# Split fetch buffers and one two-step-ahead sequence of modulation rows in a two-layer trunk

## The chip, the cores and the metric

The kernel runs on one core of a Trainium2 chip. The metric is the device time of one execution in microseconds (us); the time of a kernel is the median of its runs.

## The reference

Two layers over 512 positions of width 1024 in float32. A vector c sets, for each layer, six modulation rows of 1024 numbers:

```
ada_in = jax.nn.silu(c)
for i in range(DEPTH):
    mod = (ada_in @ w_ada[i] + b_ada[i]).reshape(b, 6, d)
    sh_m, sc_m, g_m = mod[:, 0, None, :], mod[:, 1, None, :], mod[:, 2, None, :]
    sh_f, sc_f, g_f = mod[:, 3, None, :], mod[:, 4, None, :], mod[:, 5, None, :]
    hm = rmsnorm(x, norm_mix[i]) * (1 + sc_m) + sh_m
    y = dilated_mixer(...) if i == 0 else forgetting_mixer(...)
    x = x + g_m * y
    hf = rmsnorm(x, norm_ffn[i]) * (1 + sc_f) + sh_f
    x = x + g_f * hierarchical_moe(hf, ...)
```

The dilated mixer (layer 0) projects hm to 9216 columns (three head groups of 16 heads, q, k and v each), attends within each group, merges the groups by their softmax denominators and projects back. The forgetting mixer (layer 1) is plain causal attention with a decay. The mixture of experts picks two of 16 small SwiGLU experts for each position.

## The kernel before

**Stages.** `begin` makes the first two modulation rows and the first normed input, `mixer_a` is the dilated mixer, then come the experts of layer 0, `mixer_b` and the experts of layer 1. In `mixer_a` the projection is done in four quarters Q of four heads for each group; the attention of one quarter (`far` for groups 1 and 2, `near` for group 0) is woven between the projection's matmuls by `weave`, which advances a main generator and a side generator.

**Weights.** Weights come in pieces of 128x1024 numbers (512 KB), in the order of `plan`. `Stream.fetch` puts a piece into a buffer if its counts in `held` allow one, and issues the load on SP's queue. `split` makes of a piece a high part on ScalarE (`hi`, L150) and a low part on VectorE (`lo`, L151); then the piece's buffer is free. A product is three matmuls: high by high (L302), high by low (L303), low by high (L305). A projection of 512 columns over four position blocks uses four pieces with 24 matmuls each; they are given back one after the other while the fourth block is worked on, and `done` then splits the next piece and fetches another.

**Modulation rows.** Ten more rows of `mod` are made while `mixer_a` runs. `background` lists a generator `ada` for each, and `weave` advances the first of the list at every second step of its main generator. One such row is 12 steps: eight load 128x1024 of w_ada (L400, SP's queue) and add it, times a column of silu(c), into `acc` on VectorE (L401). Then `acc` is split (L406 on ScalarE into a buffer of the weights, L407 on VectorE into `nlo`), three steps pass, and four matmuls with a column of ones add up the partitions (L413 high, L416 low). The sum goes into `nrow` and from there to memory (L423). POOL clears `acc` before (L396) and loads the bias into its first row (L397).

**Buffers.** Buffers of tag `raw` are four. Outside the experts `fetch` holds at most three for weights, and `ada` takes what is left, one at a time as a rule. The compiler's scheduler sets each engine's order from the order of the code, the dependencies and the free buffers; each engine and each queue then works in that order.

Of the kernel before, what the change touches and what calls it, by code (L numbers as in the profile page):

```python
# [8 lines left out]
F32 = mybir.dt.float32  # L9
F32R = mybir.dt.float32r  # L10
BF16 = mybir.dt.bfloat16
I32 = mybir.dt.int32
AF = mybir.ActivationFunctionType
OP = mybir.AluOpType
# [3 lines left out]
P = 128  # L18
D = 1024
S = 512  # L20
KT = D // P
# [56 lines left out]
class Stream:  # L78
# [3 lines left out]
    def __init__(self, t, pieces):  # L82
        self.t, self.pieces = t, pieces
        self.nf = self.ns = self.ng = self.nd = 0
        self.raws, self.parts = {}, {}
        self.held = {"raw": 0, "h": 0, "big": 0, "mix": 0, "row": 0, "acc": 0}
        self.moe = self.mix = self.hold = False
        self.nh = self.nrow = self.live = 0
        self.whole = {}

    def fetch(self):

        if self.nf == len(self.pieces):
            return False
        src, n, kind = self.pieces[self.nf]
        t, new = self.t, lambda pool, tag, n: pool.tile([P, 1024], F32, name=tag, tag=tag, bufs=n)
        moe = kind in ("moe", "down")
        if self.mix and kind != "" and self.held["mix"] < 6:
            tag, raw = "mix", new(t.k, "mix", 6)
        elif moe and self.held["h"] < self.nh:  # L100
            tag, raw = "h", new(t.k, "h", 8)
        elif self.moe and moe and self.held["big"] < 5:
            tag, raw = "big", new(t.k, "big", 5)
        elif moe and self.held["row"] < self.nrow:
            tag, raw = "row", new(t.k, "row", 2)
        elif self.moe and moe and self.held["acc"] < 1:
            tag, raw = "acc", new(t.w, "acc", 1)
        elif self.held["raw"] < (4 if self.moe else 3):
            tag, raw = "raw", self.t.w.tile([P, 1024], F32, name="raw", tag="raw", bufs=4)
        else:  # L110
            return False
        self.held[tag] += 1
        for ap, view in src:
            self.t.nc.sync.dma_start(out=view(raw), in_=ap)
        self.raws[self.nf] = (tag, raw)
        self.nf += 1
        return True

    def fill(self, most=10 ** 6):

        def fetch():
            while self.nf < most and self.fetch():
                pass

        fetch()
        while not self.hold and self.ns < self.nf and (self.live < 6 or self.pieces[self.ns][2] == "down"):
            self.split()
            fetch()
# [47 lines left out]
class Trunk:  # L176
# [71 lines left out]
    def finish(self):  # L248
        while self.bg:
            self.drain(self.bg.pop(0))  # L250

    def drain(self, side):
        for _ in side:
            pass
# [133 lines left out]
            if half == 0:  # L388
                self.st.fill(2)

    def ada(self, layer, j, norm, put):

        nc, i = self.nc, self.i
        acc = self.w.tile([P, D], F32, name="acc", tag="acc", bufs=1)
        row = self.nrow
        nc.gpsimd.memset(acc, 0.0)  # L396
        nc.gpsimd.dma_start(out=acc[0:1, :], in_=i["b_ada"][layer:layer + 1, j * D:(j + 1) * D])  # L397
        for kt in range(KT):
            raw = self.w.tile([P, 1024], F32, name="ada", tag="raw", bufs=4)
            nc.sync.dma_start(out=raw, in_=i["w_ada"][layer, kt * P:(kt + 1) * P, j * D:(j + 1) * D])  # L400
            nc.vector.scalar_tensor_tensor(acc, raw, self.csil[:, kt:kt + 1], acc, op0=OP.mult, op1=OP.add)  # L401
            if norm is not None and kt == KT // 2:
                nc.sync.dma_start(out=row, in_=self.bcast(norm, D, 1))
            yield
        hi, lo = self.w.tile([P, 1024], F32R, name="ada", tag="raw", bufs=4), self.nlo
        nc.scalar.activation(hi, acc, AF.Copy)  # L406
        nc.vector.tensor_tensor(lo, acc, hi.bitcast(F32), op=OP.subtract)  # L407
        for _ in range(3):
            yield
        ts = [self.bank("s")[0:1, :], self.bank("s")[0:1, :]]  # L410
        for h in range(2):
            cs = slice(h * 512, (h + 1) * 512)
            nc.tensor.matmul(ts[h], lhsT=self.one, rhs=hi[:, cs], start=True, stop=False)  # L413
        for h in range(2):
            cs = slice(h * 512, (h + 1) * 512)
            nc.tensor.matmul(ts[h], lhsT=self.one, rhs=lo[:, cs], start=False, stop=True)  # L416
        for h in range(2):
            cs = slice(h * 512, (h + 1) * 512)
            if norm is not None:
                nc.vector.scalar_tensor_tensor(row[:, cs], ts[h], 1.0, row[:, cs], op0=OP.add, op1=OP.mult)  # L420
            else:
                nc.scalar.activation(row[:, cs], ts[h], AF.Copy)
        nc.scalar.dma_start(out=put, in_=row)  # L423
        if (layer, j) == (0, 2):
            self.g_m = self.load_row(layer, 2)

    def normed(self, x, a, sh, out, sq, eng=None, after=None):

# [216 lines left out]
    def mixer_a(self, sb, xs):  # L645
# [4 lines left out]
        nc, i, st = self.nc, self.i, self.st  # L650
# [6 lines left out]
        def heads(gr):  # L657
# [15 lines left out]
            return (qt, kt, vr), turn  # L673

        def attend(near, qkv, bias, mn, den, evac):


# [82 lines left out]
        def near(Q, qkv, oqs):  # L760
            bias = sb.tile([P, 4, 256], F32, name="bias", tag="bias", bufs=2)
            nc.scalar.dma_start(out=bias, in_=bass.AP(
                tensor=ext0.tensor, offset=ext0.offset + Q * 4 * 384, ap=[[1, P], [384, 4], [1, 256]]))
            ox = sb.tile([P, NB, 264], F32, name="ox", tag="ox", bufs=1)

            def evac(hp, o):
                nc.scalar.activation(ox[:, :, 0:256].rearrange("p b (h d) -> p h b d", d=HD)[:, 2 * hp:2 * hp + 2], o, AF.Copy)

            yield from attend(True, [qkv], bias, lambda h, b: ox[:, b, 256 + h:257 + h], lambda h, b: ox[:, b, 260 + h:261 + h], evac)

            op = sb.tile([P, NB, 264], F32, name="op", tag="op", bufs=1)
            for b in range(NB):
                nc.sync.dma_start(out=near_d[Q % 2, NB - 1 - b], in_=ox[:, b, :])
            yield
            for s in range(4):
                nc.sync.dma_start(out=op[:, 3 - s, :], in_=near_d[Q % 2].rearrange("b (n r) c -> r (b n) c", r=4)[s])
            yield
            yield

            oq, st = oqs[Q]  # L780
            v = lambda n: self.sm.tile([P, NB, 4], F32, name="mg%d" % n, tag="mg%d" % n, bufs=1)
            m0, d0, m1, d1 = op[:, :, 256:260], op[:, :, 260:264], st[:, 0], st[:, 1]
            m, e0, e1, t, u = (v(n) for n in range(5))
            nc.vector.tensor_tensor(m, m0, m1, op=OP.min)
            nc.vector.tensor_tensor(e0, m, m0, op=OP.subtract)
            nc.vector.tensor_tensor(e1, m, m1, op=OP.subtract)
            nc.scalar.activation(e0, e0, AF.Exp)
            nc.scalar.activation(e1, e1, AF.Exp)
            nc.vector.tensor_tensor(t, e0, d0, op=OP.mult)
            nc.vector.tensor_tensor(u, e1, d1, op=OP.mult)  # L790
            nc.vector.tensor_tensor(t, t, u, op=OP.add)
            nc.vector.reciprocal(t, t)
            nc.vector.tensor_tensor(e0, e0, t, op=OP.mult)
            nc.vector.tensor_tensor(e1, e1, t, op=OP.mult)
            w4 = lambda a: a.unsqueeze(3).to_broadcast([P, NB, 4, HD])
            o0 = op[:, :, 0:256].rearrange("p b (h d) -> p b h d", d=HD)
            o1 = oq.rearrange("p b (h d) -> p b h d", d=HD)
            nc.gpsimd.tensor_tensor(o0, o0, w4(e0), op=OP.mult)
            nc.vector.tensor_tensor(o1, o1, w4(e1), op=OP.mult)
            nc.vector.tensor_tensor(o1, o1, o0, op=OP.add)  # L800
            yield
# [533 lines left out]
    def background(self):  # L1335
        i = self.i
        jobs = [(1, 1, i["norm_mix"][1]), (1, 0, None), (0, 2, None), (0, 3, None), (0, 4, i["norm_ffn"][0]), (0, 5, None),
                (1, 2, None), (1, 3, None), (1, 4, i["norm_ffn"][1]), (1, 5, None)]
        self.bg = [self.ada(l, j, n, self.mods[l, j:j + 1]) for l, j, n in jobs]

    def mix_in(self, layer, b, sb, x, a, sh):
        h = sb.tile([P, D], F32, name="hm", tag=("xh", "xl")[b % 2], bufs=2)
# [74 lines left out]
```

## Time and profile before

| | |
|---|---|
| median of 3 runs | 1422.62 us (1422.11 to 1424.69) |
| profiled execution | 1429.67 us, span 1427.8 us |
| PE busy | 1334.4 us, 93% |
| DVE busy | 967.1 us, 68% |
| ACT busy | 651.9 us, 46% |
| mean DMA rate | 185 GB/s |

The span is that of the recorded instructions. PE is TensorE's matmuls, PEld its weight loads, DVE VectorE, ACT ScalarE, POOL GpSimd, SP the sync engine, which here only issues loads and stores. A q behind an engine is its sequencer. "A <- B: us, n" in a view of waits says that A stood idle n times, us in total, and that the event which ended this came from B.

### The profile page before, as it was taken

How to read it: one execution, taken by the hardware profiler on the slowest of the kernel's cores; microseconds unless marked ns; L12 is line 12 of the kernel's file. 1: busy time of each engine (PE TensorE's matmuls, PEld its weight loads, DVE VectorE, ACT ScalarE, POOL GpSimd, SP SyncE). 2: the span in 40 equal slices, each digit the busy share in tenths (PEclk: the TensorE clock that was granted, in tenths of full speed). 3: DMA queues.
4: the chain of work that ended last, by engine and by line, in shares of the span. 5: the costliest groups of instructions: out<-in, count | busy, mean ns of one | idle time of the engine just before them, and what ended most of it. 6: DMA issues, size and time to landing. Idle time of an engine off the chain costs nothing. (4 is left out here: it accounts for less than half of the span.)

```text
span 1427.8 us, 20196 instructions
## 1 busy us (share of the span) xinstructions
PE 1334.4 (93%) x7165; PEld 1081.9 (76%) x7165; DVE 967.1 (68%) x1913; ACT 651.9 (46%) x1356; POOL 122.5 (9%) x120
## 2 busy tenths in 40 slices
PE   5899999999998999989999998599999999999995
PEld 4787989878996989878776665268988878766663
DVE  6875666675666676665677775486767854877772
ACT  6433544343444443453355554354554543365551
POOL 0000000000000000000032221100000000213221
PEclk9899999989999999999999999799999999999998
DMA  9465445634555545174689998513312465799991
GB/s 356 141 207 180 145 147 156 210 113 143 163 155 172 180 150 178 60 230 154 249 278 294 296 284 236 169 33 111 109 48 82 133 203 169 267 304 293 286 288 31
DMA packets 187157, 264.16 MB, mean 185 GB/s; under 512 B 23065, under 2 KB 148697, under 8 KB 187047
## 3 DMA queue, kind: packets, MB, share of 16 engines
q1 hardware_dynamic: 160742, 227.86, 49.2%
q0 software_dynamic: 8576, 16.85, 5.1%
q10 hardware_dynamic: 17728, 18.05, 4.1%
q8 instruction: 60, 0.98, 0.3%
q14 instruction: 51, 0.41, 0.1%
HBM read 249.85 MB, written 25.43 MB: 193 GB/s over the span
## 5 line engine op out<-in xcount | busy, mean ns | idle before, releaser
L302 PE MATMUL ps_pj<-hi,h 128*128 128x512 f32 (+1 forms) x1016 | 390.2, 393 | 9.6 <-ACT h L385 5.0
L303 PE MATMUL ps_pj<-lo,h 128*128 128x512 f32 (+1 forms) x1016 | 371.0, 373 | 0.0
L305 PE MATMUL ps_pj<-hi,h 128*128 128x512 f32 (+1 forms) x1016 | 288.6, 372 | 0.4 <-DVE h L463 0.4
L302 PEld LDWEIGHTS ps_pj<-hi,h 128*128 128x128 f32 x1016 | 237.5, 234 | 33.4 <-ACT h L462 7.0
L303 PEld LDWEIGHTS ps_pj<-lo,h 128*128 128x128 f32 x1016 | 239.2, 235 | 14.5 <-issue 1.1
L305 PEld LDWEIGHTS ps_pj<-hi,h 128*128 128x128 f32 x1016 | 210.7, 234 | 20.5 <-DVE h L463 1.2
L150 ACT ACTIVATE hi<-raw 128x1024 fp32r<-128x1024 f32 x126 | 132.4, 1052 | 122.6 <-PE ps_pj L305 72.0
L151 DVE TENSOR_TENSOR lo<-raw,hi 128x1024 fp32r<-128x1024 f32 x126 | 151.4, 1212 | 38.1 <-ACT hi L150 37.6
L401 DVE SCALAR_TENSOR_TENSOR acc<-ada,csil,acc 128x1024 f32<-128x1024 f32 x80 | 102.6, 1282 | 76.0 <-DMA ada<-in_w_ada 75.8
L302 PE MATMUL ps_pj<-hi,xh 128*112 128x512 f32 x256 | 103.5, 404 | 0.5 <-ACT xh L462 0.5
L303 PE MATMUL ps_pj<-lo,xh 128*112 128x512 f32 x256 | 103.3, 403 | 0.0
L305 PE MATMUL ps_pj<-hi,xl 128*112 128x512 f32 x256 | 80.3, 395 | 0.0
L1246 DVE SCALAR_TENSOR_TENSOR y<-ps_s,r_ws,g_f 112x512 f32<-112x512 f32 x64 | 47.9, 748 | 35.6 <-PE ps_s L1245 35.6
L462 ACT ACTIVATE xh<-ps_t 128x448 fp32r<-128x448 f32 x64 | 31.6, 542 | 86.4 <-PE ps_t L457 86.4
L471 DVE TENSOR_REDUCE qss<-sq 128x8 f32<-128x512 f32 x64 | 43.6, 682 | 29.9 <-ACT sq L469 29.2
L469 ACT ACTIVATE sq<-ps_pj 128x512 f32<-128x512 f32 x63 | 37.1, 588 | 55.7 <-PE ps_pj L305 53.5
L151 DVE TENSOR_TENSOR lo<-h,hi 128x1024 fp32r<-128x1024 f32 x42 | 51.1, 1222 | 15.4 <-ACT hi L150 11.2
L731 PEld LDWEIGHTS ps_o<-vr,pt 128*128 128x128 f32 x480 | 58.1, 192 | 1.4
L731 PE MATMUL ps_o<-vr,pt 128*128 128x64 f32 x480 | 57.4, 271 | 0.0
L305 PEld LDWEIGHTS ps_pj<-hi,xl 128*112 128x112 f32 x256 | 44.4, 174 | 15.2 <-DVE xl L463 0.6
L302 PEld LDWEIGHTS ps_pj<-hi,xh 128*112 128x112 f32 x256 | 44.9, 176 | 13.1 <-ACT xh L462 0.9
L936 DVE CUSTOM_DVE_ANT_0 nl<-ps_s,cums 128x128 f32<-128x128 f32 (+1 forms) x64 | 30.9, 484 | 35.2 <-PE ps_s L934 34.7
(284 smaller groups left out, 2228.4 us busy)
## 6 DMA issues: line engine op xcount, KB each, us to landing
ada<-in_w_ada SPq DMA_DIRECT2D x85, 512.0 KB
raw<-in_a_w_in SPq DMA_DIRECT2D x128, 256.0 KB
h<-in_w_gate SPq DMA_DIRECT2D x42, 256.0 KB
h<-in_w_up SPq DMA_DIRECT2D x42, 256.0 KB
mix<-in_w_gate SPq DMA_DIRECT2D x37, 256.0 KB
mix<-in_w_up SPq DMA_DIRECT2D x37, 256.0 KB
raw<-in_w_down SPq DMA_DIRECT2D x18, 512.0 KB
h<-in_w_down SPq DMA_DIRECT2D x18, 512.0 KB
```

The lines of the kernel that those rows point to most:

```text
L150: t.act = nc.scalar.activation(h, r, AF.Copy)
L151: nc.vector.tensor_tensor(l, r, h.bitcast(F32), op=OP.subtract)
L302: nc.tensor.matmul(out, lhsT=hi, rhs=wh, start=first and n == 0, stop=False)
L303: nc.tensor.matmul(out, lhsT=hi, rhs=wl, start=False, stop=False)
L305: nc.tensor.matmul(out, lhsT=lo, rhs=wh, start=False, stop=last and n == len(terms) - 1)
L401: nc.vector.scalar_tensor_tensor(acc, raw, self.csil[:, kt:kt + 1], acc, op0=OP.mult, op1=OP.add)
L462: self.nc.scalar.activation(hv, tv, AF.Copy)
L469: nc.scalar.activation(sq, ps, AF.Square)
L471: nc.vector.tensor_reduce(ss, sq.rearrange("p (h d) -> p h d", d=HD), axis=AX.X, op=OP.add)
L731: nc.tensor.matmul(held["o"][:, at:at + HD], lhsT=pt[:, a * P:(a + 1) * P], rhs=v, start=(m == 0), stop=(m == len(terms) - 1))
L936: nc.vector.tensor_tensor_reduce(out=pr[:, sl], in0=s[:, sl], in1=cums[:, hh % 2, 0:m], scale=1.0, scalar=3e38, op0=OP.add, op1=OP.min, ac ...
L1246: nc.vector.scalar_tensor_tensor(y[:, cs], yp, m["ws"][0:CAP, e:e + 1], m["g_f"][0:CAP, cs], op0=OP.mult, op1=OP.mult)
```

## The change

The four buffers `raw` become two of `raw` and two of `ada`. Weights take `raw` first, then `ada` as long as `spare` holds, which is not so from `background` until `finish`. The ten generators become one, `ada(jobs)`: its loads stand in one list, `load` issues the next of them on POOL's queue, two are issued before the first sum, and one behind each sum whose row has another for it two steps on; the next row's first two are issued behind the split and behind the matmuls. The next row's `acc` is cleared behind the split too. The four matmuls stand in the order high, high, low, low as before, with a load behind them. The load of the norm's row goes from SP's queue to ScalarE's. In `near`, the product of `op` with its weights goes from POOL to VectorE.

```
-        elif self.held["raw"] < (4 if self.moe else 3):
-            tag, raw = "raw", self.t.w.tile([P, 1024], F32, name="raw", tag="raw", bufs=4)
+        elif self.held["raw"] < 2:
+            tag, raw = "raw", new(t.w, "raw", 2)
+        elif self.spare and self.held["ada"] < 2:
+            tag, raw = "ada", new(t.w, "ada", 2)
...
-        for kt in range(KT):
-            raw = self.w.tile([P, 1024], F32, name="ada", tag="raw", bufs=4)
-            nc.sync.dma_start(out=raw, in_=i["w_ada"][layer, kt * P:(kt + 1) * P, j * D:(j + 1) * D])
-            nc.vector.scalar_tensor_tensor(acc, raw, self.csil[:, kt:kt + 1], acc, op0=OP.mult, op1=OP.add)
-            if norm is not None and kt == KT // 2:
-                nc.sync.dma_start(out=row, in_=self.bcast(norm, D, 1))
+        ahead = [(layer, j, kt) for layer, j, _ in jobs for kt in range(KT)]
+        raws = []
...
+        def load():
...
+            if ahead:
+                layer, j, kt = ahead.pop(0)
+                raw = self.w.tile([P, 1024], F32, name="ada", tag="ada", bufs=2)
+                nc.gpsimd.dma_start(out=raw, in_=i["w_ada"][layer, kt * P:(kt + 1) * P, j * D:(j + 1) * D])
+                raws.append(raw)
...
+        acc = sums(*jobs[0][:2])
+        load()
+        load()
+        yield
+        for n, (layer, j, norm) in enumerate(jobs):
+            row = self.nrow
+            for kt in range(KT):
+                nc.vector.scalar_tensor_tensor(acc, raws.pop(0), self.csil[:, kt:kt + 1], acc, op0=OP.mult, op1=OP.add)
+                if kt + 2 < KT:
+                    load()
+                if norm is not None and kt == KT // 2:
+                    nc.scalar.dma_start(out=row, in_=self.bcast(norm, D, 1))
+                yield
+            hi, lo = self.w.tile([P, 1024], F32R, name="ada", tag="ada", bufs=2), self.nlo
+            nc.scalar.activation(hi, acc, AF.Copy)
+            nc.vector.tensor_tensor(lo, acc, hi.bitcast(F32), op=OP.subtract)
+            if n + 1 < len(jobs):
+                acc = sums(*jobs[n + 1][:2])
+            load()
+            for _ in range(3):
+                yield
...
-            nc.gpsimd.tensor_tensor(o0, o0, w4(e0), op=OP.mult)
+            nc.vector.tensor_tensor(o0, o0, w4(e0), op=OP.mult)
```

On SP's queue, at the start of `mixer_a`, the program before has the weights of the projection (`raw`) and of the modulation rows (`ada`) in turn:

```order
L114 DMA raw<-in_a_w_in 128x2x256 x18
L400 DMA ada<-in_w_ada 128x1024
L403 DMA nrow<-in_norm_mix 1x1024
L400 DMA ada<-in_w_ada 128x1024 x2
L114 DMA raw<-in_a_w_in 128x2x256 x4
L400 DMA ada<-in_w_ada 128x1024 x5
L114 DMA raw<-in_a_w_in 128x2x256 x6
```

The changed program has weights of the projection alone there, the first four pieces of them over both kinds of buffer:

```order
L117 DMA raw<-in_a_w_in 128x2x256 x4
L117 DMA ada<-in_a_w_in 128x2x256 x4
L117 DMA raw<-in_a_w_in 128x2x256 x4
L117 DMA ada<-in_a_w_in 128x2x256 x4
L117 DMA raw<-in_a_w_in 128x2x256 x12
L117 DMA raw<-in_a_w_in 128x4x256 x2
L117 DMA raw<-in_a_w_in 128x2x256 x24
```

The 80 loads of modulation weights have gone from this queue, and no load of weights stands behind one of them any more. On POOL's queue of the changed program they stand between the clearing of `acc` and the bias of each row (first and second row):

```order
L411 MEMSET acc 128x1024
L412 DMA acc<-in_b_ada 1x16x64
L406 DMA ada<-in_w_ada 128x1024 x9
L411 MEMSET acc 128x1024
L412 DMA acc<-in_b_ada 1x16x64
L406 DMA ada<-in_w_ada 128x1024 x8
```

The first load of a row has moved ahead of the clearing, the other seven stand behind it. On ScalarE, for the third row, the program before has the split of the sum (`ada<-acc`) and, behind its matmuls, the copy into `nrow` four rows apart:

```order
L406 ACTIVATE ada<-acc 128x1024
L702 ACTIVATE nl,ox<-nl,ox 128x128
L702 ACTIVATE nl,ox<-nl,ox 128x256
L469 ACTIVATE sq<-ps_pj 128x512
L422 ACTIVATE nrow<-ps_s 1x512 x2
```

In the changed program 25 rows lie between the two; these are the first of them:

```order
L429 ACTIVATE ada<-acc 128x1024
L774 DMA bias<-ext_432 128x8x128
L225 ACTIVATE rs_y_1371<-qss 128x8
L217 ACTIVATE pt<-ps_t 128x512
L226 ACTIVATE rs_y_1371<-rs_y_1371 128x8
L568 ACTIVATE vr<-ps_pj 128x256
```

The split has moved forward, by 21 rows, against the copy that follows its matmuls.

## Rows read from the trace of the kernel before

**Rows 1.** The page: the span, and TensorE's busy time, share and instructions.

```profile
span 1427.8 us, 20196 instructions
PE 1334.4 (93%) x7165; PEld 1081.9 (76%) x7165; DVE 967.1 (68%) x1913; ACT 651.9 (46%) x1356; POOL 122.5 (9%) x120
```

**Rows 2.** Stretches: length, busy us by engine, granted clock, DMA share, GB/s.

```profile
60.00:160.00 100.00, 95.12 (x486) 84.26 (x485) 69.35 (x136) 41.11 (x97) 4.31 (x6) 1.00 0.54 166
160.00:260.00 100.00, 97.41 (x538) 90.75 (x538) 63.98 (x141) 43.39 (x110) 2.88 (x4) 0.98 0.51 162
260.00:360.00 100.00, 93.89 (x534) 81.54 (x533) 66.20 (x134) 41.90 (x105) 4.82 (x5) 0.93 0.47 148
360.00:460.00 100.00, 95.12 (x496) 84.64 (x496) 68.75 (x135) 40.94 (x100) 4.81 (x5) 0.98 0.52 164
460.00:560.00 100.00, 98.27 (x576) 91.47 (x575) 70.00 (x152) 48.29 (x119) 1.45 (x2) 1.00 0.51 162
```

**Rows 3.** Waits from 60 to 560 us: total us, times, longest us.

```profile
DVE acc L401 <- DMA ada<-in_w_ada: 75.8, 52, 4.0
ACT hi L150 <- DMA raw<-in_a_w_in: 29.0, 6, 9.2
PE ps_s L413 <- ACT ada L406: 12.3, 6, 3.2
PE ps_t L711 <- ACT nl L702: 3.0, 3, 1.3
PE ps_t L666 <- DVE qn L477: 2.3, 3, 1.2
```

**Rows 4.** The timeline from 252 to 293 us: start, us, engine, line; idle before.

```profile
252.96 0.34 SPq L400 DMA_DIRECT2D ada<-in_w_ada  x1
...
257.92 1.28 DVE L401 SCALAR_TENSOR_TENSOR acc<-ada,csil,acc 128x1024 f32<-128x1024 f32 x1 [3.09 <-DMA ada<-in_w_ada]
...
259.23 14.53 SPq L400 DMA_DIRECT2D ada<-in_w_ada  x5
...
265.08 1.28 DVE L401 SCALAR_TENSOR_TENSOR acc<-ada,csil,acc 128x1024 f32<-128x1024 f32 x1
...
269.85 1.28 DVE L401 SCALAR_TENSOR_TENSOR acc<-ada,csil,acc 128x1024 f32<-128x1024 f32 x1 [3.10 <-DMA ada<-in_w_ada]
...
280.62 1.06 ACT L150 ACTIVATE hi<-raw 128x1024 fp32r<-128x1024 f32 x1 [9.24 <-DMA raw<-in_a_w_in]
...
283.97 1.42 PE L711 MATMUL ps_t<-ident,nl 128*128 128x128 f32 x6 [0.81 <-ACT nl L702]
...
290.91 1.06 ACT L406 ACTIVATE ada<-acc 128x1024 fp32r<-128x1024 f32 x1 [3.63 <-DVE acc L401]
...
292.02 1.01 PE L413 MATMUL ps_s<-ada,one 128*1 128x512 f32 x2 [2.49 <-ACT ada L406]
```

**Rows 5.** A shorter stretch around that wait, columns as in rows 2.

```profile
290.00:295.00 5.00, 2.98 (x8) 1.68 (x9) 3.19 (x5) 1.53 (x2) 1.42 (x2) 0.50 0.13 28
```

**Rows 6.** Tile ada: instructions, ns least, median, most, first and last start.

```profile
L401 DVE SCALAR_TENSOR_TENSOR acc<-ada,csil,acc x80: 1271/1284/1289, 68.0 to 551.3; 128x1024 f32<-128x1024 f32 x80
```

**Rows 7.** POOL's gathers: their row among the groups, and of the DMA issues.

```profile
L1207 POOL DMA_INDIRECT xr<-hf_d,r_ii x32 | 38.3, 1198 | 43.1 <-PE ps_t L457 12.7 <-DMA h<-in_w_down 9.2 <-DMA h<-in_w_gate 9.2
xr<-hf_d,r_ii POOLq DMA_INDIRECT x32, 8.1
```

**Rows 8.** DMA issues of the dilated mixer's projection weights, KB each.

```profile
raw<-in_a_w_in SPq DMA_DIRECT2D x128, 256.0 KB
raw<-in_a_w_in SPq DMA_DIRECT2D x8, 512.0 KB
```

**Rows 9.** The timeline at the end of the first quarter's merge.

```profile
260.85 1.90 POOL L798 TENSOR_TENSOR op<-op,mg 128x1024 f32<-128x1024 f32 x1 [10.44 <-DVE mg L794]
260.88 2.95 DVE L799 TENSOR_TENSOR big<-big,mg 128x1024 f32<-128x1024 f32 x1
...
263.93 1.23 DVE L800 TENSOR_TENSOR big<-big,op 128x1024 f32<-128x1024 f32 x1
```

More of the change, by code (lines that the diff above doesn't have):

```diff
@@ L85, in __init__ @@
         self.raws, self.parts = {}, {}
-        self.held = {"raw": 0, "h": 0, "big": 0, "mix": 0, "row": 0, "acc": 0}
+        self.held = {"raw": 0, "h": 0, "big": 0, "mix": 0, "row": 0, "acc": 0, "ada": 0}
         self.moe = self.mix = self.hold = False
+        self.spare = True
         self.nh = self.nrow = self.live = 0
@@ L250, in finish @@
             self.drain(self.bg.pop(0))
+        self.st.spare = True
     def drain(self, side):
@@ L389, in begin, with ada @@
                 self.st.fill(2)
-    def ada(self, layer, j, norm, put):
+    def ada(self, jobs):
         nc, i = self.nc, self.i
[L394 to L397, printed above, removed]
-        for kt in range(KT):
-            raw = self.w.tile([P, 1024], F32, name="ada", tag="raw", bufs=4)
-            nc.sync.dma_start(out=raw, in_=i["w_ada"][layer, kt * P:(kt + 1) * P, j * D:(j + 1) * D])
-            nc.vector.scalar_tensor_tensor(acc, raw, self.csil[:, kt:kt + 1], acc, op0=OP.mult, op1=OP.add)
-            if norm is not None and kt == KT // 2:
-                nc.sync.dma_start(out=row, in_=self.bcast(norm, D, 1))
-            yield
[L405 to L425, printed above, removed]
@@ new lines, in ada, with sums @@
+        ahead = [(layer, j, kt) for layer, j, _ in jobs for kt in range(KT)]
[6 more added lines that the diff above has]
+                raws.append(raw)
+        def sums(layer, j):
+            acc = self.w.tile([P, D], F32, name="acc", tag="acc", bufs=1)
+            nc.gpsimd.memset(acc, 0.0)
+            nc.gpsimd.dma_start(out=acc[0:1, :], in_=i["b_ada"][layer:layer + 1, j * D:(j + 1) * D])
+            return acc
@@ new lines, in ada @@
+        acc = sums(*jobs[0][:2])
[19 more added lines that the diff above has]
+                yield
+            ts = [self.bank("s")[0:1, :], self.bank("s")[0:1, :]]
+            for part in (hi, lo):
+                for h in range(2):
+                    cs = slice(h * 512, (h + 1) * 512)
+                    nc.tensor.matmul(ts[h], lhsT=self.one, rhs=part[:, cs], start=part is hi, stop=part is lo)
+            load()
+            for h in range(2):
+                cs = slice(h * 512, (h + 1) * 512)
+                if norm is not None:
+                    nc.vector.scalar_tensor_tensor(row[:, cs], ts[h], 1.0, row[:, cs], op0=OP.add, op1=OP.mult)
+                else:
+                    nc.scalar.activation(row[:, cs], ts[h], AF.Copy)
+            nc.scalar.dma_start(out=self.mods[layer, j:j + 1], in_=row)
+            if (layer, j) == (0, 2):
+                self.g_m = self.load_row(layer, 2)
+            yield
@@ L1338, in background @@
                 (1, 2, None), (1, 3, None), (1, 4, i["norm_ffn"][1]), (1, 5, None)]
-        self.bg = [self.ada(l, j, n, self.mods[l, j:j + 1]) for l, j, n in jobs]
+        self.bg = [self.ada(jobs)]
+        self.st.spare = False
     def mix_in(self, layer, b, sb, x, a, sh):
```

## The prediction

> **What bounds the kernel now.** I read the page first: TensorE is busy 93% of a span of 1427.8 us [rows 1], so time can only come from its gaps and from stretches in which its clock is low. The change acts in the dilated mixer, so the second view is the table of stretches from 60 to 560 us [rows 2], where the ten modulation rows are made. TensorE is busy 95.12, 97.41, 93.89, 95.12 and 98.27 us of 100: 20.2 us of gaps. The granted clock averages 1.00, 0.98, 0.93, 0.98 and 1.00. A stretch that is busy b us at a share c of the full clock would do the same work in b times c, so b(1 - c) is lost: 1.9 + 6.6 + 1.9 = 10.4 us, and since the column has two digits, somewhere from 8.0 to 12.8 us. I go on with 8. All that a better order of this stage's loads can give is thus about 28 us of the 500, unless other stages move.
>
> The third view, the waits of that stretch [rows 3], says whose the gaps are. Of 20.2 us, 12.3 are six waits of L413, the matmul that adds up a modulation row, for ScalarE's split of it. VectorE waited 75.8 us, 52 times, for modulation weights at L401.
>
> The fourth view is the timeline into one of those waits [rows 4], to be read from its end. TensorE stood 2.49 us at 292.02 for the split of 290.91, which had waited 3.63 us for the sum on VectorE. The sum was late because its loads go one at a time: the sum of 257.92 ends at 259.20, the next load is issued at 259.23, and the one behind the sum of 265.08 (it ends at 266.36) is in at 269.85. The landing takes 269.85 - 266.36, about 3.5 us, and 257.92 - 252.96, about 5.0 us, in the other instance. A step of the sum therefore costs 3.5 to 5.0 us and 1.28 us of VectorE, 4.8 to 6.3 us. The sums of 80 loads start from 68.0 to 551.3 us [rows 6], which is 9 rows of 12 steps and 7 more, 115 steps, so a step of the program is given 483.3 / 115 = 4.2 us. The chain cannot keep up, and the three steps of slack behind it are used up in six rows of ten. The same queue carries the projection's weights: SP's five loads from 259.23 take 14.53 us, nearly all of it waiting, and ScalarE then stands 9.24 us at 280.62 for a piece of weights, behind which TensorE stands at 283.97. In the 5 us around the wait at 292 TensorE's clock is at 0.50 [rows 5], the lower of its two levels (1.2 GHz of 2.4), after a stretch with gaps; this is where the 0.93 of [rows 2] comes from.
>
> **The change, part by part.**
>
> *Two loads ahead.* With two buffers, a load is issued when the sum two steps before it has ended. For two sums the cycle is one landing, one issue and one sum. Landing on POOL's queue is not in the trace for a load of this kind. From below I take SP's 3.5 us, from above the gathers on POOL's queue, 112 rows of 4 KB with 8.1 us to landing in the median and 1.2 us of POOL each [rows 7], measured beside the experts' loads. So a sum every (3.5 + 1.28) / 2 = 2.4 us to (8.1 + 1.2 + 1.28) / 2 = 5.3 us, against the 4.2 us that a step has. A plain load in a stage whose DMA engines are half busy [rows 2] is nearer to SP's loads: at 5.0 + 1.2 the cycle is 3.7 us. Then the sums keep up, L413 finds its split ready, and 12.0 of the 12.3 us go. The slow clock hangs on these gaps: 7 of the 8 us go with them. Of the waits at L711 and L666, 5.3 us, which stand behind ScalarE and VectorE held up by loads, I take half, 2.5 us.
>
> *POOL's share.* 80 loads at about 1.2 us are 96 us of POOL in 500, beside some 18 us of other work [rows 2]; it is covered by POOL's idle time. The clearing of `acc` stands in this queue ahead of seven loads of its row and waits for the low part of the sum before it. The loads behind it are needed a step and more after the matmuls, three steps later, so this wait is covered; without the three steps it would cost a landing for each row.
>
> *Two buffers for weights instead of three.* Here the change takes something away. A buffer is free again after the high part, 1.06 us [rows 4], the low part, 1.23 us as for L800 of the same size [rows 9], and a new landing, 3.5 to 5.0: 5.8 to 7.3 us. The projection has 128 / 2 + 8 = 72 pieces [rows 8], 18 bursts of four. In a burst two pieces lie ready; the third is asked for two parts of 6 matmuls later, at 95.12 us for 486 matmuls [rows 2] 2.4 us. ScalarE may so stand 3.4 to 4.9 us in each burst, 61 to 88 us in all, in place of 29.0 [rows 3]. How much of this TensorE feels: today 29.0 us of such waits go with 3.0 us at L711, or 5.3 with L666, 10 to 18%. The 32 to 59 us more are then 3 to 11 us. I take 4, near the lower end, because SP no longer stands behind modulation loads and the scheduler puts other rows of ScalarE between the splits.
>
> *The norm's rows on ScalarE's queue.* Three loads; two stand close behind the store from the same buffer, and ScalarE would wait there. Between nothing and twice a landing, 10 us of ScalarE, of which TensorE feels a tenth or so: 0.5 us.
>
> *The product in `near` on VectorE.* Four times POOL's 1.90 us go and VectorE gets a product. L799, started beside L798 and of the same kind as L800, takes 2.95 us and L800 1.23 [rows 9]. I read the difference as L799 waiting for POOL's instruction, so both products on VectorE take 2.46 us instead of 2.95. VectorE is busy below 70% here, so the term is nothing; were it 1.23 us more each time, 5 us of VectorE would still lie beside the projection's matmuls. The Trainium skill says so too (SBUF — State Buffer, Who interferes with whom): a VectorE instruction with two SBUF inputs contends with a GpSimd one that reads SBUF. By that rule, the trace agrees: 2.95 beside 1.90.
>
> *The other stages.* Outside the mixer weights have four buffers instead of three in `mixer_b` and in the transitions. The time there I leave as it is, within 2 us either way.
>
> The sum: 12.0 + 7 + 2.5 - 4 - 0.5 = 17.0 us. The profiled execution of 1429.7 us becomes 1412.7. The median of the runs is 7.1 us below it, so I forecast 1422.6 - 17.0, about 1405.5 us; I write 1405. What a measurement here can tell from no change is 0.2%, 2.8 us.
>
> **The rivals.**
>
> *POOL's queue is slow.* If a load there lands as late as a gather, 8.1 us, a sum comes every 5.3 us, and VectorE waits 80 times 1.1 us, 88 us, more than today's 75.8. Eight such cycles are 42 us of the 46 us that 11 steps have, so L413 is late only in the shorter rows: half of 12.3 and of the clock come back, 10 us, nothing at L711 and L666, less 4.5: 1417 us. For it: [rows 7]. Against it: those loads are gathers and run when the experts' weights fill the engines. The Trainium skill has a rule for this (SBUF — State Buffer, the trap "DVE blocks DMA"): descriptors of GpSimd's loads are written by GpSimd itself, which some VectorE copies lock out. No run so far shows it. In rows of this kernel one such block is at most one VectorE instruction, 1.28 us a load, 0.6 us a sum, and 3.7 becomes 4.4 us, a little over a step: two thirds of the forecast's gain, 1411 us. I give that 0.05 of this rival's chance.
>
> *Weights come too late (slower).* In each of the 18 bursts ScalarE stands for the third and fourth piece, and behind it stand the squares and exponents on which TensorE's transposes wait. The price is the share that reaches TensorE. With 59 us more of waits, the gain of 21.5 us is gone at 36%; at 55% the loss is 32 us and the time 1433 us. For it: the one wait of 9.24 us did reach TensorE [rows 4]. Against it: ScalarE's waits of this kind are 29.0 us today and TensorE's behind them at L711 3.0, and SP's queue is freed.
>
> *Nothing changes.* L413 may find its sum ready and TensorE stand for something else in the same place, as the engines behind it are 70% and 45% busy: 1422 us. Against it: no other wait of [rows 3] is a quarter of L413's.
>
> **How the numbers follow.** Forecast, gains of 12 to 30 us: 0.60. Slow queue on POOL, 1411 to 1419 us: 0.17. Nothing: 0.08. Weights too late: 0.15, a third of it within 0.2% or a small gain, the rest slower. So faster by over 0.2%: 0.60 + 0.17 + 0.03 = 0.80; within: 0.08; slower: 0.12. The range of 8 in 10 takes in the forecast with its terms' bounds (28 us at most, 2 us from other stages) and the slow queue: 1392 to 1419 us. The forecast's own range is 1392 to 1411.
>
> **What would show it.** Right: VectorE's wait for `ada` falls from 75.8 us below 25, no wait of TensorE for the split of `acc` over 1 us, the clock at 0.98 or more in all five stretches, SP's queue without waits for VectorE's sums. The term for the weights is seen in ScalarE's wait for `raw`, today 29.0 us, and in what L711 and L666 then wait. Wrong: `ada` waits above 75 us mean a slow POOL queue; new waits of TensorE for VectorE or ScalarE late in each burst mean that two buffers are too few; a shift in the experts' stages would come from the order of fetches there, which I count as nothing.

## The result, and the profile after

The changed kernel takes 1415.91 us in the median of 6 runs (1413.09 to 1419.05); the kernel before, run beside it, 1424.27 (1422.11 to 1428.55). The ratio is 0.9948, 95% interval 0.9931 to 0.9964: faster by 7.4 us, 5 to 10. The direction and the range held. The forecast gain, 17 us, is more than twice what came.

The page of the profiled execution (1415.43 us), to be held against [rows 1]: busy time by engine, then the group of the modulation sums, their loads, and the two kinds of load with the median us to landing.

```profile
PE 1329.2 (94%) x7165; PEld 1081.8 (77%) x7165; DVE 960.4 (68%) x1917; ACT 651.4 (46%) x1356; POOL 154.7 (11%) x196
...
L422 DVE SCALAR_TENSOR_TENSOR acc<-ada,csil,acc 128x1024 f32<-128x1024 f32 x80 | 102.6, 1282 | 74.3 <-DMA ada<-in_w_ada 66.1
...
L406 POOL DMA_DIRECT2D ada<-in_w_ada x80 | 42.4, 530 | 341.9 <-DVE acc L422 246.1
...
ada<-in_w_ada POOLq DMA_DIRECT2D x80, 512.0 KB, 4.1
raw<-in_a_w_in SPq DMA_DIRECT2D x120, 256.0 KB, 3.8
```

A load on GpSimd's queue lands in 4.1 us, far from the 8.1 us of the gathers [rows 7], and yet VectorE still waits 66.1 us for loads. The same stretches as [rows 2]:

```profile
60.00:160.00 100.00, 92.47 (x466) 81.37 (x466) 71.64 (x136) 39.92 (x95) 17.10 (x30) 0.98 0.60 180
160.00:260.00 100.00, 97.25 (x543) 90.33 (x540) 65.42 (x144) 44.16 (x108) 11.10 (x20) 0.98 0.54 170
260.00:360.00 100.00, 94.76 (x545) 83.06 (x544) 66.72 (x137) 41.81 (x108) 11.67 (x21) 0.95 0.49 152
360.00:460.00 100.00, 99.23 (x534) 89.84 (x534) 70.42 (x147) 44.58 (x111) 11.94 (x21) 1.00 0.52 164
460.00:560.00 100.00, 98.66 (x562) 91.86 (x561) 65.02 (x153) 45.30 (x112) 5.17 (x9) 1.00 0.50 155
```

TensorE's gaps are 500 less the five busy times, 17.6 us against 20.2, and busy time times one less the clock gives 8.5 us of slow clock against 10.4 (both to the column's two digits). The waits from 60 to 560 us (total, times, longest), against [rows 3]:

```profile
DVE acc L422 <- DMA ada<-in_w_ada: 66.1, 45, 4.7
...
ACT hi L153 <- DMA raw<-in_a_w_in: 35.1, 16, 5.4
...
PE ps_t L692 <- DVE qn L503: 6.4, 6, 2.9
...
PE ps_t L692 <- DVE rs_t L227: 2.7, 1, 2.7
...
PE ps_t L737 <- ACT pt L217: 2.6, 2, 2.4
PE ps_s L440 <- DVE ox L726: 2.4, 2, 2.2
```

The add-up matmul (now L440) waits for no split any more; those 12.3 us are gone. But TensorE waits for VectorE in other places: L692 and L737 are the L666 and L711 of before. How that hangs together is seen in the timeline around one of them:

```profile
349.77 1.28 DVE L422 SCALAR_TENSOR_TENSOR acc<-ada,csil,acc 128x1024 f32<-128x1024 f32 x1 [2.30 <-DMA ada<-in_w_ada]
...
352.88 0.51 ACT L728 ACTIVATE nl<-nl,ox 128x256 f32<-128x256 f32 x1 [5.27 <-DVE ox L726]
...
353.25 0.39 PE L440 MATMUL ps_s<-ada,one 128*1 128x512 f32 x1 [2.19 <-DVE ox L726]
```

VectorE stood 2.30 us for a load; its attention work (L726) came later by that, and TensorE stood 2.19 us behind it. A late load holds up whatever is queued behind the sum on VectorE, not the sum's own reader alone.

Why are loads still late? The timeline of one row's change to the next (L429 makes the high part of a finished sum):

```profile
126.56 0.53 POOL L406 DMA_DIRECT2D ada<-in_w_ada  x1 [5.68 <-DVE acc L422]
127.33 1.04 ACT L429 ACTIVATE ada<-acc 128x1024 fp32r<-128x1024 f32 x1
134.03 1.29 DVE L422 SCALAR_TENSOR_TENSOR acc<-ada,csil,acc 128x1024 f32<-128x1024 f32 x1 [1.71 <-DMA acc<-in_b_ada]
135.61 0.54 POOL L406 DMA_DIRECT2D ada<-in_w_ada  x1 [3.99 <-DVE acc L422]
139.61 1.28 DVE L422 SCALAR_TENSOR_TENSOR acc<-ada,csil,acc 128x1024 f32<-128x1024 f32 x1 [1.08 <-DMA ada<-in_w_ada]
141.19 0.53 POOL L406 DMA_DIRECT2D ada<-in_w_ada  x1 [5.04 <-DVE acc L422]
...
141.73 0.39 PE L440 MATMUL ps_s<-ada,one 128*1 128x512 f32 x1 [1.63 <-DVE st L726]
...
143.30 0.53 POOL L406 DMA_DIRECT2D ada<-in_w_ada  x1 [1.58 <-PE ps_s L440]
```

At 127.33 the high part of the sum is written into one of the two `ada` buffers, and it stays there until TensorE, whose queue is full of projections, comes to L440 at 141.73 (for the last 1.63 us TensorE stood for VectorE). Until then one buffer serves the loads: that of 135.61 waits for the sum of 134.03, that of 141.19 for the sum of 139.61. The load of 143.30 is the first into the buffer that L440 gives back. This row is a mild case. Taken from the start of L429 to the end of the second L440 of the high part, the ten rows held the buffer for 3 to 45 us, seven of them for over 30, and up to six of the next row's eight sums were made meanwhile. Over all rows 45 of 79 loads were issued only when the sum just before theirs had ended (one ahead, below), 33 when the one before that had (two ahead); before the change 62 and 12, worked out from the starts of L422 and L406 one by one.

### The profile page after: what moved, and what is told of

Read it like the earlier page. It is cut to its first block, busy times and chain, and to the rows that moved or that the text cites. A ratio compares the mean times of both kernels' runs of the same rounds, so it can differ in the third digit from the quotient of the medians.

```text
span 1413.6 us, 20206 instructions
## 1 busy us (share of the span) xinstructions
PE 1329.2 (94%) x7165; PEld 1081.8 (77%) x7165; DVE 960.4 (68%) x1917; ACT 651.4 (46%) x1356; POOL 154.7 (11%) x196
## 5 line engine op out<-in xcount | busy, mean ns | idle before, releaser
L154 DVE TENSOR_TENSOR lo<-raw,hi 128x1024 fp32r<-128x1024 f32 x98 | 119.6, 1222 | 54.9 <-ACT hi L153 51.3
L422 DVE SCALAR_TENSOR_TENSOR acc<-ada,csil,acc 128x1024 f32<-128x1024 f32 x80 | 102.6, 1282 | 74.3 <-DMA ada<-in_w_ada 66.1
L153 ACT ACTIVATE hi<-raw 128x1024 fp32r<-128x1024 f32 x98 | 103.6, 1057 | 94.4 <-DMA raw<-in_a_w_in 50.9
L406 POOL DMA_DIRECT2D ada<-in_w_ada x80 | 42.4, 530 | 341.9 <-DVE acc L422 246.1
L497 DVE TENSOR_REDUCE qss<-sq 128x8 f32<-128x512 f32 x64 | 43.6, 682 | 38.9 <-ACT sq L495 38.4
L495 ACT ACTIVATE sq<-ps_pj 128x512 f32<-128x512 f32 x63 | 37.1, 590 | 64.8 <-PE ps_pj L309 55.6
L154 DVE TENSOR_TENSOR lo<-mix,hi 128x1024 fp32r<-128x1024 f32 x41 | 50.2, 1232 | 12.5 <-ACT hi L153 11.9
L309 PEld LDWEIGHTS ps_pj<-hi,xl 128*112 128x112 f32 x256 | 44.5, 174 | 15.2 <-DVE xl L489 0.6
L154 DVE TENSOR_TENSOR lo<-h,hi 128x1024 fp32r<-128x1024 f32 x38 | 46.1, 1223 | 14.4 <-ACT hi L153 13.6
```

Source lines behind the costliest of these rows:

```text
L153: t.act = nc.scalar.activation(h, r, AF.Copy)
L154: nc.vector.tensor_tensor(l, r, h.bitcast(F32), op=OP.subtract)
L309: nc.tensor.matmul(out, lhsT=lo, rhs=wh, start=False, stop=last and n == len(terms) - 1)
L406: nc.gpsimd.dma_start(out=raw, in_=i["w_ada"][layer, kt * P:(kt + 1) * P, j * D:(j + 1) * D])
L422: nc.vector.scalar_tensor_tensor(acc, raws.pop(0), self.csil[:, kt:kt + 1], acc, op0=OP.mult, op1=OP.add)
L495: nc.scalar.activation(sq, ps, AF.Square)
```

## The experiments

Each ratio is to the kernel before on the same chip, under 1 where the version is faster, with its 95% interval in brackets. Waits are those from 60 to 560 us. `a` marks an edit to the changed kernel, `b` one to the kernel before.

**Theory A: the high part holds the second buffer.** Three edits of a.

`hi_ring`: the high part in one of the six buffers of the weights' high parts.

```
- hi, lo = self.w.tile([P, 1024], F32R, name="ada", tag="ada", bufs=2), self.nlo
+ hi, lo = self.w.tile([P, 1024], F32R, name="ahi", tag="hi", bufs=6), self.nlo
- (self.live < 6 or ...
+ (self.live < (6 if self.spare else 5) or ...
```

> The changed kernel, with the high part of each modulation sum in a buffer of the weights' six 'hi' buffers (weights run five pieces ahead in place of six while modulation rows are made), so that both 'ada' buffers serve loads alone. Theory A (the high part holds the second buffer until TensorE adds it up, so that most loads are only one sum ahead): VectorE's wait for modulation weights from 60 to 560 us falls from 66 us to under 30, the loads issued right behind the sum before them from 45 of 79 to under 15, TensorE's gaps and slow clock give back 4 to 8 us more: 1408 to 1412 us against 1415.9. Rival B (GpSimd's queue delivers late): the waits stay above 55 us and the time at 1414 to 1417. Rival C (weights in two buffers are late, and that sets TensorE's gaps): modulation waits fall, the time stays at 1414 to 1417.

Measured: 1430.85 us, 1.0055 [1.0036, 1.0074]: slower, against every theory. The timeline has one stall:

```profile
114.65 1.01 PE L440 MATMUL ps_s<-ahi,one 128*1 128x512 f32 x2 [14.19 <-ACT ahi L429]
```

In its first row all eight loads were one sum ahead, as if another tile held the second buffer (which one the trace doesn't say); in the other nine rows all were two ahead. From the 420th to the 1680th projection matmul it took 385.2 us, the changed kernel 392.2; but `live_5`, next, whose ratio is the changed kernel's, took 386.5, so single profiles differ by that much. Not a test yet.

`live_5`: the second line of that edit alone.

> The changed kernel, with weights split five pieces ahead in place of six while modulation rows are made, and nothing else: the cost of the room that hi_ring takes. Theory A: 1415 to 1418 us, within 0.2% of the changed kernel, as TensorE waits for no weights there. Rival C (weights are late): fewer pieces ahead cost more, 1418 to 1425, and ScalarE's wait for raw weights falls as its splits are asked for later.

Measured: 1413.22, 0.9947 [0.9925, 0.9970], as the changed kernel: one piece of lead less costs nothing that can be told.

`hi_ring2`: hi_ring with the lead cut (`self.lim = 5`) only from the fourth sum of the first row on. `hi_ring3`: the same, and back to six after each row's add-up matmuls.

> hi_ring lost some 17 us once, ahead of its first add-up matmul (one wait of 14.2 us), where its first eight loads were one sum ahead; from the 420th projection matmul to the 1680th it took 385.2 us, the changed kernel 392.1. Here the weights' lead is cut from six pieces to five only from the fourth sum of the first row on, so that both 'ada' buffers should be free of weights in the first row as they are in the changed kernel. Theory A (the high part holds the second buffer): no wait over 5 us ahead of the first add-up, modulation waits from 60 to 560 us under 30 us, 1404 to 1411 us. Rival (the gain between the two marks was the variance of single profiles): 1413 to 1418 us, as live_5 and the changed kernel.

> hi_ring2, with the weights' lead at five pieces only from the fourth sum of each row until its add-up matmuls, else six. Theory A: as hi_ring2, 1403 to 1411 us; the two differ by what a sixth piece is worth, under 2 us by live_5. Rival (variance): 1413 to 1418 us.

Measured: 1404.87, 0.9881 [0.9849, 0.9913], and 1406.65, 0.9880 [0.9857, 0.9903]. Of 79 loads, 78 were two ahead in both. The timeline of hi_ring2 (L408 the loads, L424 the sums and L154 the weights' split there) and its waits:

```profile
141.49 1.28 DVE L424 SCALAR_TENSOR_TENSOR acc<-ada,csil,acc 128x1024 f32<-128x1024 f32 x1
143.07 0.53 POOL L408 DMA_DIRECT2D ada<-in_w_ada  x1 [2.08 <-DVE acc L424]
144.36 1.28 DVE L424 SCALAR_TENSOR_TENSOR acc<-ada,csil,acc 128x1024 f32<-128x1024 f32 x1
145.94 0.53 POOL L408 DMA_DIRECT2D ada<-in_w_ada  x1 [2.34 <-DVE acc L424]
147.23 1.29 DVE L424 SCALAR_TENSOR_TENSOR acc<-ada,csil,acc 128x1024 f32<-128x1024 f32 x1 [0.37 <-DMA ada<-in_w_ada]
```
```profile
ACT hi L154 <- DMA raw<-in_a_w_in: 40.3, 20, 6.1
...
DVE acc L424 <- DMA ada<-in_w_ada: 25.1, 27, 3.1
```

The load of 143.07 serves the sum of 147.23, with another sum between. VectorE's waits fall from 66.1 to 25.1 us, and 0.9948 - 0.9881 = 0.67%, 9.5 us, comes back. From 60 to 560 us TensorE's gaps fall from 17.6 to 12.3 us and its slow clock, worked out as above (0.98 in two of the five stretches of hi_ring2), from 8.5 to 3.9, 9.9 us together. Theory A holds. The stretch of 500 us as one row, in the changed kernel, in hi_ring2 and in hi_ring3 (columns as in [rows 2]):

```profile
60.00:560.00 500.00, 482.38 (x2641) 436.46 (x2640) 339.20 (x713) 215.78 (x531) 56.97 (x100) 0.98 0.53 164
```
```profile
60.00:560.00 500.00, 487.70 (x2704) 447.11 (x2703) 342.14 (x718) 219.24 (x538) 57.16 (x100) 0.99 0.55 166
```
```profile
60.00:560.00 500.00, 484.83 (x2690) 442.04 (x2690) 339.96 (x716) 218.91 (x538) 57.17 (x100) 1.00 0.54 165
```

`yield_1`: a with `range(1)` in place of `range(3)` steps between split and add-up.

> The changed kernel, with one step in place of three between the split of a modulation sum and the matmuls that add it up, so that TensorE frees the buffer of the high part some 8 us sooner. Theory A: VectorE's wait for modulation weights from 60 to 560 us falls from 66 to about 45 us, and the time to 1411 to 1415 us, unless TensorE now waits for the split as it did before the change (12.3 us of waits there), which would cost up to 10 us: 1418 to 1426. Rival B (GpSimd's queue delivers late): waits for modulation weights stay at 60 to 70.

Measured: 1419.11, 0.9987 [0.9968, 1.0006], waits 55.6 us, 23 loads one ahead, read from an execution of 1431.36 us, 12 over the median. The buffer comes free sooner, as Theory A has it, but the kernel is slower than the changed one, and TensorE stands 5.5 us for the split again. The edit also takes two steps out of each row, so the last sum ends at 454 us and not 528 and the loads come closer together: inconclusive.

**What the loads cost in all.** `one_load`: a with one piece for all sums. `traffic`: all loads issued, all sums from the first piece.

```
one_load:  - if ahead:                        traffic:  - raws.append(raw)
           + if len(ahead) > 79:                        + if not raws: raws.append(raw)
both:      - raws.pop(0)   + raws[0]
```

> The changed kernel, which fetches one piece of modulation weights and uses it for all 80 partial sums (79 of the 80 loads, 40 MB, are left out, so the modulation rows are not the reference's); every other instruction stays. It shows what the waits for these loads cost in all. Theory A: VectorE waits for no modulation weights, TensorE's gaps from 60 to 560 us fall from 17.6 to about 6 us, the clock is 1.00, and the time is 1396 to 1404 us. Rival D (TensorE's gaps come from VectorE's order and work, not from the loads): 1411 to 1416 us, with gaps of 14 us or more.

> The changed kernel with all 80 loads issued, but all sums made from the first piece, so that no sum waits for a load (the modulation rows are not the reference's; the other loads are written over unread). Beside one_load (1385.8) it shows whether the modulation loads cost by being waited for or by their traffic. Theory A (the waits cost): under 1392 us, projections from the 420th to the 1680th matmul in 371 to 376 us, VectorE waits for no modulation weights. Rival E (traffic: two queues share the transfers, so weights come later): 1400 to 1412 us, with ScalarE's waits for raw weights at 35 us from 60 to 560 as in the changed kernel, against 24.5 in one_load.

Measured: one_load 1385.78, 0.9754 [0.9726, 0.9782], below even Theory A's range. TensorE is busy 497.78 of 500 us there at a clock of 1.00:

```profile
60.00:560.00 500.00, 497.78 (x2789) 456.27 (x2789) 351.73 (x736) 226.18 (x554) 14.97 (x21) 1.00 0.29 87
```

So waits, slow clock and traffic of these loads cost the changed kernel 0.9948 - 0.9754 = 1.94%, 28 us. The kernel before is 35 us slower than one_load, but one_load has the change's other parts in it too, so the 35 don't test the 28 us that the prediction read off its stretches. traffic: 1454.23, 1.0215 [1.0179, 1.0251], outside both ranges. It failed as a test: the unread loads go into the buffer that the high part wants, and ScalarE stood 52.2 us for them. Waits and traffic were thus not told apart this way.

**Rival B: GpSimd's queue.** `seq_on_sync`: a with the loads on SP's queue, still two ahead in the code.

```
- nc.gpsimd.dma_start(out=raw, in_=i["w_ada"]...
+ nc.sync.dma_start(out=raw, in_=i["w_ada"]...
```

> The changed kernel with the modulation loads, two ahead as now, on SP's queue in place of GpSimd's. Theory A (the buffer, not the queue, sets the waits): modulation waits from 60 to 560 us at 60 to 85, and 1414 to 1422 us; a load that waits there for its buffer holds back the weight loads behind it, so ScalarE's raw waits may rise from 35 to 45 us. Rival B (GpSimd's queue is slow to deliver): modulation waits fall below 50 us and the time below 1412.

`both`: that and hi_ring2.

> hi_ring2 and seq_on_sync together: the high part in a weights' buffer, the loads two ahead on SP's queue. If each removed waits of its own (the buffer: loads one sum ahead; the queue: 0.29 us more from a sum's end to the load's issue, 0.16 us more to its landing, on the 45 loads that are on the path), the second gain shrinks once loads are two ahead, as the lag is then covered: 1399 to 1405 us, modulation waits from 60 to 560 us under 20 us. If GpSimd's queue costs in another way (by how it shares the transfers with the weights, ScalarE's raw waits 32 us on it against 19 on SP's between the marks), the gains add up: 1391 to 1398 us with raw waits of 20 us or less.

Measured: seq_on_sync 1403.69, 0.9864 [0.9843, 0.9884]; both 1395.24, 0.9813 [0.9787, 0.9839], the fastest version that makes the right rows, 27 us below the kernel before. Waits of seq_on_sync, then of both:

```profile
DVE acc L422 <- DMA ada<-in_w_ada: 42.9, 40, 3.7
...
ACT hi L153 <- DMA raw<-in_a_w_in: 28.6, 19, 4.2
```
```profile
ACT hi L154 <- DMA raw<-in_a_w_in: 29.1, 21, 5.6
...
DVE acc L424 <- DMA ada<-in_w_ada: 23.6, 23, 3.3
```

I had expected nothing of the queue, and it is worth 12 us: the waits and the time are those of Rival B, not of Theory A, so the buffer is not the only cause. In seq_on_sync 43 loads are one ahead, nearly as many as the 45 on GpSimd's queue. What differs is the load itself: from the end of the sum that frees the buffer to the issue 0.29 us on GpSimd and 0.03 on SP, and from issue to the waiting sum 4.16 and 4.00 us (medians), 0.42 us together. The Trainium skill gives a difference of this size (DMA: Bandwidth & Descriptors, Specifications: a first byte after some 1 us through GpSimd, 0.6 through the other queues). The trace bears it out in the total alone: 0.26 of the 0.42 us lie ahead of the issue, and the rest is not steady from run to run, 4.26 us from issue to sum in hi_ring2 on GpSimd's queue and 4.33 in `both` on SP's.

Sorted by lead, the waits differ only where nothing covers the load. VectorE waited for 29 loads one ahead, 43.3 us, on GpSimd's queue and for 20, 18.6 us, on SP's; for loads two ahead 22.8 and 24.4 us. By my estimate 29 x 0.42 = 12 of these 25 us are the longer load; where the others come from is not shown.

With two loads ahead the 0.42 us should be covered, and VectorE's waits are indeed equal (25.1 and 23.6). Yet hi_ring2 and both differ by 10 us, and ScalarE's waits for weights by 11. One place is plain. SP's queue in hi_ring2, with ScalarE's next split, then SP's in both:

```profile
233.72 2.04 SPq L803 DMA_DIRECT2D near_d<-ox  x4
241.32 0.80 SPq L806 DMA_DIRECT2D op<-near_d  x2
242.22 0.90 SPq L118 DMA_DIRECT2D raw<-in_a_w_in  x2
```
```profile
247.04 1.06 ACT L154 ACTIVATE hi<-raw 128x1024 fp32r<-128x1024 f32 x1 [5.50 <-DMA raw<-in_a_w_in]
```
```profile
238.60 2.86 SPq L118 DMA_DIRECT2D raw<-in_a_w_in  x4
241.56 1.83 SPq L806 DMA_DIRECT2D op<-near_d  x4
```

With the modulation loads gone from SP's queue, the scheduler puts the read-back of near's sums (L806) ahead of the weights' loads. It waits for near's store (L803) to land, until 241.32, and the weights behind it come late. `near_back_pool` (from hi_ring2) and `near_back_pool_after` (from a) put the read-back on GpSimd's queue (`nc.sync` to `nc.gpsimd` in that one line).

> hi_ring2 with the read-back of near's sums (op from near_d, four loads in each of the four near stages) on GpSimd's queue, so that no weights' load stands behind it on SP's. Theory F (GpSimd's queue cost 10 us there because the weights' loads, left alone on SP's queue, were put behind that read-back, which waits some 5 us for its transfer): ScalarE's raw waits from 60 to 560 us fall from 40 to under 30 us, none over 4 us near 247 and 396 us, and the time is 1397 to 1401 us against 1404.9. Rival (the issue on GpSimd itself, 0.29 us, and its 0.53 us of work): no change, 1403 to 1408, or more where a modulation load stands behind the read-back on GpSimd's queue.

> The changed kernel with the same read-back on GpSimd's queue. Theory F: 1407 to 1412 us against 1415.9, with raw waits from 35 to under 28 us; modulation loads, mostly one sum ahead here, lose up to 5 us behind the read-back, so the gain may be half. Rival: 1415 to 1420.

Measured: 1400.13, 0.9867 [0.9832, 0.9902], raw waits 36.7 us, the wait near 247 now 2.5 and that near 396 3.4; and 1413.22, 0.9958 [0.9932, 0.9984], raw waits 38.9. The two long waits (5.5 and 6.1 us in hi_ring2) are shorter, but neither interval shows a gain over its base, and raw waits stay far above the forecast of under 30 and under 28 us. The read-back is at most a part; what else makes weights late while GpSimd's queue carries the other loads stays open.

**The other parts, each alone on b, and added up.**

```
division_alone:     - elif self.held["raw"] < (4 if self.moe else 3): ... tag="raw", bufs=4
                    + elif self.held["raw"] < 2: ...   and   elif self.spare and self.held["ada"] < 2: ...
                    ada's tiles: - tag="raw", bufs=4   + tag="ada", bufs=2
near_on_vector:     - nc.gpsimd.tensor_tensor(o0, o0, w4(e0), op=OP.mult)   + nc.vector. ...
near_on_gpsimd (a): the reverse
division_near:      the first two
division_near_row:  and norm's rows: - nc.sync.dma_start   + nc.scalar.dma_start
```

> The kernel before with the four fetch buffers divided, two for projection and two for modulation weights, and nothing else of the change: loads of modulation weights stand ahead of each sum on SP's queue as before. The prediction put the division at 4 us of cost, between 3 and 11: 1425 to 1434 us against 1423. The rival that the division itself serves (a modulation load no longer waits behind a weight's buffer): 1412 to 1420 us, with modulation waits from 60 to 560 us down from 75.8 to under 60.

> The kernel before with the one product of near (4 instructions of 1.90 us on GpSimd) on VectorE (4 of 1.23 us), and nothing else. The prediction put it at 0 us: 1420 to 1426 us. Rival D (the gain of the change comes from it): 1413 to 1418 us.

> The changed kernel with near's product back on GpSimd, whose queue now carries the loads: four times a load that comes due waits up to 1.9 us behind it. Theory A: 1414 to 1419 us. Rival D: 1420 us or more.

> The kernel before with the division and with near's product on VectorE, loads ahead of each sum on SP's queue as before. If the two parts add up: 1409 to 1411 us where before has 1423, which leaves about 6 us to the sequence and the norm's rows in seq_on_sync (ratio 0.9864). If the product's gain was that of one order of execution: 1413 to 1415.

> division_near with the norm's rows on ScalarE's queue: seq_on_sync without the sequence. The prediction put the rows at a gain of 0.5 us less nothing (a cost of 0.5 in its sum): within 2 us of division_near. If the rows hold back loads on SP's queue: 3 to 6 us less, so that the sequence itself is worth nothing.

| kernel | median us | ratio | 95% |
|---|---|---|---|
| division_alone | 1413.74 | 0.9936 | 0.9914 to 0.9958 |
| near_on_vector | 1417.96 | 0.9969 | 0.9953 to 0.9985 |
| division_near | 1407.95 | 0.9914 | 0.9879 to 0.9948 |
| division_near_row | 1404.88 | 0.9887 | 0.9852 to 0.9923 |
| seq_on_sync (and the sequence) | 1403.69 | 0.9864 | 0.9843 to 0.9884 |
| the change (and GpSimd's queue) | 1415.91 | 0.9948 | 0.9931 to 0.9964 |
| near_on_gpsimd | 1421.21 | 0.9987 | 0.9963 to 1.0010 |

The division alone gives as much as the whole change, as the rival in its expectation had it; division_near is under both ranges expected of it. Waits of division_alone:

```profile
DVE acc L405 <- DMA ada<-in_w_ada: 46.6, 33, 4.0
ACT hi L153 <- DMA raw<-in_a_w_in: 28.9, 16, 4.7
```

VectorE's fall from 75.8 to 46.6 us, ScalarE's stay at 29, and TensorE's 12.3 us for the split are gone here too. In it 42 loads are one ahead, the 43 of seq_on_sync: SP's queue runs ahead of VectorE by itself, and as soon as modulation weights have two buffers of their own the old code loads as far ahead as the new sequence. From division_alone to seq_on_sync each step's interval overlaps the next, so what product, rows and sequence add there, 3 to 4 us each by the ratios, is not shown step by step; the last step, onto GpSimd's queue, loses 12 us, and that is shown. Near's product is seen from two sides: alone it gains 0.31%, 4.4 us, and taken back out of the change (near_on_gpsimd) it loses 0.39%, 5.6 us, with intervals that just touch. Both times came out as Rival D said, so it has a share in the gain of the change, though the division alone has more.

## Why the prediction was right or wrong

**The step that failed first** is in *Two loads ahead*: "With two buffers, a load is issued when the sum two steps before it has ended". It was so for 33 of 79 loads. The two buffers serve three uses, and the third, the high part, sits in one of them until TensorE reaches the add-up. The diff shows that tile, and I did not count how long it stays: not the three steps of the code, some 13 us at 4.2 each, but over 30 us in seven rows of ten. In place of the forecast "`ada` below 25 us" came 66.1; hi_ring2, where the step is true, has 25.1 and 1404.9 us, the number predicted, though partly by other terms than mine.

**The terms.** L413's 12.0 us went, as said. Of the clock's 7 us some 2 came, with 17.6 us of gaps left. That the slow clock hangs on these gaps was a looser link than I took it for: hi_ring3 has 15.2 us of gaps (500 less 484.83) at a clock of 1.00 in all five stretches. The 2.5 us at L711 and L666 became a loss, as VectorE's late sums now reach TensorE there (L692, L737, L440).

***POOL's share*** was called covered. A load takes 0.53 us of POOL, not 1.2. The landing, 4.1 us, was inside my bounds and nearer to the lower, and the cycle for two loads, (4.16 + 0.29 + 1.28) / 2 = 2.9 us, better than the 3.7 that I used. But 45 loads were only one ahead, 29 of these were waited for, and the queue costs 12 us. The wait for the clearing of `acc` was not wholly covered either: VectorE stood four times, 8.2 us in all, for the bias behind it (1.71 us at 134.03 above), and never before the change. The rival *POOL's queue is slow* named 1417 us and nearly met it, by another road: not a late landing and waits above 75, but in part 0.42 us a load. That GpSimd's descriptors would be locked out by VectorE is not seen: 69 loads were issued 0.29 to 0.35 us behind the sum that freed them, and all 80 took POOL 0.53 to 0.55 us.

***Two buffers for weights instead of three***, -4 us with bounds of -3 and -11, has the wrong sign: division_alone gains 9 (6 to 12), with ScalarE's raw waits at 28.9 us as before. I had priced only what it takes from the weights, and put what it gives the modulation loads to the sequence's account. The rival *Weights come too late* is refuted by that run.

***The product in near***, 0 us, is worth 4.4 (2 to 7). The reading of L799 was right: on its own (now L825) it takes 1.22 us and not 2.95, each time. The line of before, then of after:

```profile
L799 DVE TENSOR_TENSOR big<-big,mg x4: 2948/2948/2953, 260.9 to 674.4; 128x1024 f32<-128x1024 f32 x4
```
```profile
L825 DVE TENSOR_TENSOR big<-big,mg x4: 1217/1218/1219, 263.6 to 671.4; 128x1024 f32<-128x1024 f32 x4
```

The Trainium skill's rule (SBUF — State Buffer, Who interferes with whom), by which a VectorE instruction with two SBUF inputs contends with a GpSimd instruction that reads SBUF, agrees. Four instances save VectorE 4 x (2.95 + 1.23) - 4 x (1.23 + 1.22 + 1.22) = 2 us; where the rest comes from I have not found.

***The norm's rows***, -0.5 us: the ratios say 3 to 4 us of gain, the intervals nothing.

The steps of the table, in ratios: division 9, product 3, rows and sequence 7 together, queue -12: 7 us, against 12 + 7 + 2.5 - 4 - 0.5. They are steps of one chain from the kernel before to the change, so they add up to its gain whatever each of them is worth elsewhere. That the total fell inside my range was in part luck: the division's wrong sign and the queue's cost partly cancelled. The chances have a slip too: a third of 0.15 is 0.05, so with 0.03 of it under faster, within should be 0.10 and slower 0.10.

## What to carry to other kernels

Before counting on a load n steps ahead, list every tile that takes a buffer of that ring and how long each is held, in time of the engine that frees it; a tile that waits for the busiest engine leaves a ring of two with one buffer. Try the division of a shared ring by itself first: a queue that runs ahead of its consumer prefetches without new code. Loads of this kind whose length is on the path were 12 us cheaper on SP's queue than on GpSimd's; and when loads leave a queue, see what the scheduler then puts in front of those that stay.

## What the runs showed of the hardware that was not expected

A 512-KB load was issued 0.29 us after the sum that freed its buffer on GpSimd's queue, 0.03 us on SP's. From issue to the waiting sum no steady difference is seen: medians of 4.16 (the change) and 4.26 us (hi_ring2) on GpSimd's queue, 4.00 (seq_on_sync) and 4.33 us (both) on SP's. A product of two SBUF operands on VectorE (128x1024) took 2.95 us beside GpSimd's, 1.22 us without. Without modulation loads (one_load) the clock was 1.00 in all five stretches and TensorE's gaps 2.2 us of 500, so the slow clock of this stage (8.5 us after the change) is not there of itself. The sum of the gaps doesn't set it either: 15.2 us of them in hi_ring3 went with 1.00 in all five stretches, 10.7 us in division_alone with 0.95 and 0.97 in two.
